# A decoder block in split float32: sums of weights in their quarters' place, four places for split pieces, pairs by sums and plain pairs in turn

## The chip, the core and the metric

The kernel runs on one core of one Trainium2 chip. The core has engines with queues of their own: TensorE (PE in the profile) multiplies matrices, VectorE (DVE), ScalarE (ACT) and GpSimd (POOL) work element by element, and SyncE (SP) starts most of the transfers from HBM. The metric is the device time of one execution in microseconds, and the output must agree with the reference.

## The reference

One layer of a decoder on 256 tokens of 2048 features, all in float32: a feed-forward network (FFN), a mixer of two kinds of attention, and a second FFN, each with a norm ahead and a norm behind it.

```
D_MODEL = 2048
SEQ = 256
D_FF = 5632

def swiglu(x, w_gate, w_up, w_down):
    return (jax.nn.silu(x @ w_gate) * (x @ w_up)) @ w_down

f = swiglu(rmsnorm(x, ffn1_pre_g[l]), ffn1_w_gate[l], ffn1_w_up[l], ffn1_w_down[l])
x = x + FFN_RES_SCALE * rmsnorm(f, ffn1_post_g[l])
h = rmsnorm(x, mix_pre_g[l])
proj = h @ w_in[l]
...
x = x + rmsnorm(o @ w_out[l], mix_post_g[l])
f = swiglu(rmsnorm(x, ffn2_pre_g[l]), ffn2_w_gate[l], ffn2_w_up[l], ffn2_w_down[l])
x = x + FFN_RES_SCALE * rmsnorm(f, ffn2_post_g[l])
```

The change is about the last product of `swiglu`, hidden features (5632) times `w_down`, and about how every weight reaches PE.

## The kernel before, in words

**Split operands.** PE multiplies in a rounded 32-bit format, fp32r. To keep float32 accuracy each operand is split into a high part (the value rounded to fp32r) and a low part (the rest), and three products are added up: high by high, high by low, low by high. The weights are split on the chip. The class `Weights` keeps a list of blocks of 1 MB, each loaded by SP into a ring of three `raw` tiles (`RAW`), and a list of pieces of 1024 columns (in all) per partition. `split_next` makes one piece: ACT copies it to `whi` (line 136), DVE subtracts to `wlo` (line 141). There is a ring of three places for them (`PARTS`), so that piece n can be split only when piece n-3 has been multiplied; `get(i)` asks for splits up to i + 2 and for loads up to two blocks ahead.

**Gate and up.** For each of 22 pairs of feature blocks the weights are PE's stationary operand and the 256 tokens (high and low side by side, 512 columns) its moving one; a piece is 8 matmuls of 512 columns and 8 of 256. Short steps on ACT and DVE, held in a list `todo` and run one entry after each piece (`step`), join the two halves, apply the gate, and split the result for the next product.

**Down.** This product is done in two halves of 11 pairs of feature blocks each, and in each half in two column pairs (2 x 512 of the 2048 output columns). `Down.run` goes through the pairs. A plain pair is two pieces, each of 12 matmuls of 512 columns: 24 for the pair. Four pairs of each half, those in `BY_SUMS`, go by a scheme with seven products in place of eight (a form of Strassen's): the 2 x 2 blocks of hidden features and of weights are added and subtracted, and 21 matmuls do the pair. Their weights come in four pieces, with 6, 3, 6 and 6 matmuls; two of these are sums of the four quarters of a raw block, made on DVE (lines 102, 106, 110) into two tiles of their own, `sum..0` and `sum..1`. `TERMS` says which of the seven sums (of hidden features) meets which quarter and which product bank it goes to. After the last pair by sums, `middle` puts the seven products together on DVE and ACT; after the last pair `finish` adds the plain banks. The second column pair of the second half ends in a tail, in which the last three pairs go one column chunk after the other, so that the norm behind it can begin (`handover`), and the next stage's weights are already split while PE works off held pieces (`take_over`). In these stretches between `ordered()` and `order.close()` the order on the engines is as the program writes it. Elsewhere a scheduler puts each engine's instructions in order by when it believes them to be ready; on the chip each engine then works its queue off strictly in that order.

**Slots.** `slots` is a set of 30 tiles of 4 KB per partition that activations, sums and intermediate results take and give back.

Of the kernel before, what the change touches and what calls it, by code (L numbers as in the profile page):

```python
# [10 lines left out]
F32 = mybir.dt.float32  # L11
# [6 lines left out]
P = 128  # L18
# [8 lines left out]
CH = 512  # L27
# [33 lines left out]
class Weights:  # L61

    RAW, PARTS, WIDTH = 3, 3, 1024

    def __init__(self, nc, pool):
        self.nc, self.pool = nc, pool
        self.blocks, self.raw, self.pieces, self.parts = [], {}, [], {}
        self.loaded = self.split = 0  # L70
        self.sums = None

    def block(self, w, k0, nk, c0, cols, step=None):
        src = w[k0 * P:(k0 + nk) * P, c0:c0 + cols].rearrange("(k p) f -> p k f", p=P)
# [17 lines left out]
    def add_sums(self, w, k0, c0):  # L92


        b = self.block(w, k0, 2, c0, 2 * CH)
        quarters = lambda raw: raw.rearrange("p k (c f) -> p (k c) f", c=2)
        ends = lambda raw: quarters(raw)[:, 0::3]
        eng = self.nc.vector

        def first(raw):  # L100
            t = self.sums[0]
            eng.tensor_sub(t, ends(raw), quarters(raw)[:, 1:2].to_broadcast([P, 2, CH]))

        def second(raw):
            t, u = self.sums
            eng.tensor_add(u[:, 0], quarters(raw)[:, 3], t[:, 0])

        def third(raw):
            u = self.sums[1]
            eng.tensor_sub(u[:, 1], quarters(raw)[:, 2], u[:, 0])  # L110

        return [
            self.piece(b, 2, CH, ends, first),
            self.piece(b, 1, CH, lambda raw: quarters(raw)[:, 2:3], second),
            self.piece(b, 2, CH, lambda raw: self.sums[0], third),
            self.piece(b, 2, CH, lambda raw: self.sums[1], None),
        ]

    def load_to(self, i):
# [54 lines left out]


A11, A12, A22, S1, S3, S2, S4 = range(7)
TERMS = (((0, A11, "1"), (1, S4, "3")), ((0, A12, "2"),), ((0, S1, "5"), (1, S3, "7")), ((0, S2, "6"), (1, A22, "4")))

PLAIN = (("2", "3"), ("4", "X"))

BY_SUMS = (0, 2, 5, 7)
KP = KF // 4


# [1 line left out]
def hybrid_layer(ctx: ExitStack, tc: tile.TileContext, a):  # L186
    nc = tc.nc
    const = ctx.enter_context(tc.tile_pool(name="const", bufs=1))
    slots = Slots(ctx.enter_context(tc.tile_pool(name="slots", bufs=1)), 30)
    wpool = ctx.enter_context(tc.tile_pool(name="wpool", bufs=2))  # L190
    tmp = ctx.enter_context(tc.tile_pool(name="tmp", bufs=2))
    psum = ctx.enter_context(tc.tile_pool(name="psum", bufs=8, space=bass.MemoryType.PSUM))
# [4 lines left out]
    W = Weights(nc, wpool)  # L197
    todo = deque()

    def step():  # L200

        if todo:
            run_all(todo.popleft())
# [34 lines left out]
    def plan_down(n, half, w):  # L238


        for u in range(2):
            end = KP - 3 if (half, u) == (1, 1) else KP
            plan["down", n, half, u] = []
            for p in range(end):
                k, c0 = 2 * (half * KP + p), u * 2 * CH
                plan["down", n, half, u].append((p, W.add_sums(w, k, c0) if p in BY_SUMS else W.add(w, k, 2, c0, 2 * CH)))
        if half == 1:
# [79 lines left out]
    def row_gain(name):  # L327
        g = a[name]
        t = const.tile([P, D], F32, tag="rows", name=f"r_{name}")
        tc.keep_in_program_order(  # L330
            nc.sync.dma_start(t, bass.AP(tensor=g.tensor, offset=g.offset, ap=[[0, P], [1, D]])))
        return t
# [367 lines left out]
    def ffn(n, pre, row_name, end_of):  # L700
# [4 lines left out]
        def put_h(p, f, u, g):  # L705

            if p % KP not in BY_SUMS:
                if f == 0:
# [98 lines left out]
        class Down:  # L807


            def __init__(self, half, u):  # L810
                self.half, self.c = half, (2 * u, 2 * u + 1)
                self.ps, self.done = {}, {}
                self.pairs = plan["down", n, half, u]
                sums = len(BY_SUMS)
                self.n = {x: 3 * sums for x in "1234567"}
# [25 lines left out]
            def run(self):  # L841
                for p, ids in self.pairs:
                    q = self.half * KP + p
                    for m, i in enumerate(ids):
                        part = W.get(i)
                        if p in BY_SUMS:
                            self.sums(*hx[q], part, TERMS[m])
                        else:
                            for t in range(NT):
                                self.plain(hx[q][:, m], part, 0, t)  # L850
                        step()
                    if p == BY_SUMS[-1]:
                        self.middle()
                    if self.c[0]:
                        slots.give(*([f"hi{n}_{q}", f"ho{n}_{q}"] if p in BY_SUMS else [f"h{n}_{q}"]))

# [46 lines left out]

        for half in range(2):
            for fp in range(half * KP, (half + 1) * KP):
                if fp % KP == KP - 1:
                    W.sums = [slots.take([P, 2, CH], F32, f"sum{n}{half}{m}") for m in range(2)]
                gate_up(fp)
            if half == 0:
                post = Post(f"f{n}", row_gain(row_name), half=True)  # L910
            else:
                slots.give(*pre.names)
                more = [slots.take([P, 2, CH], F32, f"more{n}{m}") for m in range(2)]
            for u in range(2):
                d = Down(half, u)
                d.run()
                if (half, u) != (1, 1):
                    for c, t in ((1, 0), (0, 0), (0, 1), (1, 1)):
                        d.finish(c, t)
            slots.give(*(f"sum{n}{half}{m}" for m in range(2)))  # L920
        d.tail(end_of(post))
        slots.give(*(f"more{n}{m}" for m in range(2)), *(f"h{n}_{KF // 2 - 3 + m}" for m in range(3)))
        return post
# [11 lines left out]
    def end_f1(post):  # L935
        return handover(post, next_pre("pre", G[:, G_MIXPRE:G_MIXPRE + KD], "mix", post))

    post1 = ffn(1, pre1, "ffn1_post_g", end_f1)


# [233 lines left out]
    def end_f2(post):  # L1174
# [26 lines left out]
        return end  # L1201

    ffn(2, mix["pre2"], "ffn2_post_g", end_f2)


# [26 lines left out]
```

## Time and profile before

| what | value |
|---|---|
| time, median of 3 runs (lowest, highest) | 1900.07 us (1899.29, 1900.13) |
| the profiled execution: its time, its span | 1898.98 us, 1897.2 us |
| PE busy, matmuls | 1863.5 us (98 %), 9802 |
| DVE busy | 1336.7 us (70 %) |
| ACT busy | 968.6 us (51 %) |
| POOL busy | 105.1 us (6 %) |
| read from HBM | 350 MB, 186 GB/s over the span |
| mean granted clock of PE | 0.995 |

The span runs from the first to the last instruction of the profiled execution; its time is a little longer, and the medians are of other executions. Busy shares are means over the whole span. Matmuls overlap in the record (one of 512 columns is listed with about 0.39 us and starts some 0.23 us after the one before), so lost time on PE is read from starts. In a row of a timeline the bracket at the end gives the idle time of the engine just ahead of the row and what ended it.

### The profile page before, as it was taken

Reading aid. Unit: us, or ns where it says so; the run is one execution under the profiler, and the core shown is the slowest. Engines: PE = TensorE matmul, PEld = TensorE weight load, DVE = VectorE, ACT = ScalarE, POOL = GpSimd, SP = SyncE. Lnnn points to the kernel's source line nnn. Section 1 sums busy time; section 2 is a strip of 40 time slices with the busy share of each in tenths; the row PEclk is TensorE's granted clock in tenths of the full one; section 3 lists DMA queues with packets and bytes.
Section 4 is the critical chain, followed back from the end, with each engine's and each line's share of the span. In section 5 each row is a group of like instructions: output and inputs, shape, how many; then the busy total and the mean of one; then the engine's idle time right before and its main releaser. Section 6 shows DMA issues by size and latency. Waiting matters only on the chain.

```text
span 1897.2 us, 25219 instructions
## 1 busy us (share of the span) xinstructions
PE 1863.5 (98%) x9802; PEld 1590.2 (84%) x9802; DVE 1336.7 (70%) x1966; ACT 968.6 (51%) x1411; POOL 105.1 (6%) x92
## 2 busy tenths in 40 slices
PE   9999999999999998999999998999999999999997
PEld 8888887888888776788888887888887788888875
DVE  6666688766666788656786558766688766666797
ACT  6444455444444555655555446544454544444554
POOL 0000000000000001100353003000000000000001
PEclk9999999999999999999999999999999999999999
DMA  7556565556565554555545555555555655555563
GB/s 252 194 181 196 180 220 196 193 187 195 183 197 181 199 198 145 187 173 168 163 158 171 189 173 177 178 194 185 192 208 188 210 187 191 184 194 185 187 205 112
DMA packets 260120, 353.73 MB, mean 186 GB/s; under 512 B 5856, under 2 KB 219040, under 8 KB 259616
## 3 DMA queue, kind: packets, MB, share of 16 engines
q1 hardware_dynamic: 259552, 351.30, 55.9%
q8 instruction: 77, 1.26, 0.3%
q0 software_dynamic: 272, 0.75, 0.1%
q14 instruction: 43, 0.35, 0.1%
q10 hardware_dynamic: 176, 0.07, 0.0%
HBM read 350.00 MB, written 2.10 MB: 186 GB/s over the span
## 4 chain that ended last, share of the span: by engine, by line
PE 89%; DVE 8%; ACT 2%; issue 1%; POOL 0%; DMA 0%; DVEq 0%; ACTq 0%; POOLq 0%
PE p L496 34%; PE p L505 17%; PE d L825 16%; PE pq L496 5%; PE pw L515 4%; PE pv L515 4%; DVE wlo L141 3%; PE d_X L825 3%; PE pq L505 3%; ACT whi L136 1%; DVE xn L676 1%; DVE fg_f L877 1%; PE po L1026 0%; PE xt_f L459 0%; ACT sqd L368 0%
## 5 line engine op out<-in xcount | busy, mean ns | idle before, releaser
L141 DVE TENSOR_TENSOR wlo<-raw,whi 128x1024 fp32r<-128x1024 f32 (+1 forms) x653 | 784.0, 1205 | 464.5 <-ACT whi L136 452.2
L136 ACT CAST whi<-raw 128x1024 fp32r<-128x1024 f32 (+1 forms) x657 | 674.9, 1028 | 715.1 <-PE p L496 355.6
L496 PE MATMUL p<-xg_f,whi 128*128 128x512 f32 x2784 | 699.1, 392 | 0.0
L496 PEld LDWEIGHTS p<-xg_f,whi 128*128 128x128 f32 x2784 | 500.3, 189 | 89.2
L505 PEld LDWEIGHTS p<-xg_f,wlo 128*128 128x128 f32 x2816 | 384.7, 190 | 27.6
L505 PE MATMUL p<-xg_f,wlo 128*128 128x256 f32 x2816 | 393.8, 282 | 0.0
L825 PE MATMUL d<-whi,h 128*128 128x512 f32 x672 | 211.3, 390 | 0.0
L825 PEld LDWEIGHTS d<-whi,h 128*128 128x128 f32 x672 | 126.1, 188 | 27.0
L496 PE MATMUL pq<-xg_mix,whi 128*128 128x512 f32 x512 | 131.8, 399 | 0.0
L825 PE MATMUL d<-wlo,h 128*128 128x512 f32 x336 | 115.4, 392 | 2.4 <-DVE wlo L141 2.4
L141 DVE TENSOR_TENSOR wlo<-sum,whi 128x1024 fp32r<-128x1024 f32 x64 | 78.3, 1223 | 50.7 <-ACT whi L136 49.8
L496 PEld LDWEIGHTS pq<-xg_mix,whi 128*128 128x128 f32 x512 | 92.2, 189 | 16.9
L136 ACT CAST whi<-sum 128x1024 fp32r<-128x1024 f32 x64 | 67.4, 1052 | 71.7 <-PE d_X L825 46.2
L515 PE MATMUL pv<-whi,xg_mix 128*128 128x512 f32 x256 | 84.3, 400 | 1.7 <-ACT xg_mix L425 1.7
L825 PE MATMUL d_X<-whi,h 128*128 128x512 f32 x224 | 85.6, 389 | 0.0
L655 ACT COPY right<-p 128x256 f32<-128x256 f32 x176 | 60.2, 370 | 43.4 <-DVE u L657 43.4
L825 PE MATMUL d<-wlo,hi 128*128 128x512 f32 x224 | 76.6, 412 | 1.5 <-DVE wlo L141 0.8
L825 PEld LDWEIGHTS d<-wlo,h 128*128 128x128 f32 x336 | 62.0, 188 | 18.9 <-DVE wlo L141 5.1
L515 PE MATMUL pw<-whi,om 128*128 128x512 f32 x256 | 75.1, 391 | 0.0
L505 PEld LDWEIGHTS pq<-xg_mix,wlo 128*128 128x128 f32 x512 | 69.8, 190 | 5.3
L825 PE MATMUL d<-whi,ho 128*128 128x512 f32 x224 | 72.1, 391 | 0.0
L825 PE MATMUL d<-whi,hi 128*128 128x512 f32 x224 | 71.8, 390 | 0.0
(199 smaller groups left out, 1569.9 us busy)
## 6 DMA issues: line engine op xcount, KB each, us to landing
raw<-in_ffn_w_down_dram SPq DMA_DIRECT2D x86, 1024.0 KB, 4.9
raw<-in_ffn_w_gate_dram SPq DMA_DIRECT2D x84, 1024.0 KB, 5.1
raw<-in_ffn_w_up_dram SPq DMA_DIRECT2D x84, 1024.0 KB, 5.1
raw<-in_w_in_dram SPq DMA_DIRECT2D x48, 1024.0 KB, 5.2
raw<-in_w_out_dram SPq DMA_DIRECT2D x16, 1024.0 KB, 5.0
raw<-in_ffn_w_up_dram SPq DMA_DIRECT2D x8, 512.0 KB, 3.8
raw<-in_ffn_w_gate_dram SPq DMA_DIRECT2D x7, 512.0 KB, 3.6
xn<-in_x_dram SPq DMA_DIRECT2D x8, 256.0 KB, 6.1
```

What stands on the lines that cost most here:

```text
L136: self.nc.scalar.copy(hi, raw)
L141: eng.tensor_sub(lo[:, k0:k1], raw[:, k0:k1], hi[:, k0:k1].bitcast(F32))
L496: nc.tensor.matmul(p, wh, x, start=k == 0, stop=False)
L505: nc.tensor.matmul(p[:, :T], lo[:, j, f * P:(f + 1) * P], xs(k)[:, 0, :], start=False, stop=k == KD - 1)
L515: nc.tensor.matmul(ps[c], y, w[:, j, c * CH:(c + 1) * CH], start=first and n == 0, stop=last and n == 2)
L655: nc.scalar.copy(t, ps[:, T:])
L676: nc.vector.scalar_tensor_tensor(x, f, self.z[t], x, op0=ALU.mult, op1=ALU.add)
L825: nc.tensor.matmul(self.ps[x], y, w, start=m == 1, stop=m == self.n[x])
L877: nc.vector.tensor_add(f, self.ps[PLAIN[t][c]], f)
```

## The change

Three things change together. The sums of weights are written into the quarters of the raw block itself (q0 - q1 into q0, q3 - q1 into q1, then q3 + q0 into q3, and q2 - q3 into q2), so the two `sum` tiles and their slots go: 28 slots are left. The operation over two quarters becomes two over one. The third piece now reads quarters 0 and 1, the fourth quarters 2 and 3, which turns round the two terms of the last piece. The space freed is given to a fourth place in the ring of split pieces: piece n waits for piece n-4, and `get` asks for splits up to i + 3. And `BY_SUMS` becomes 0, 2, 4, 6 in place of 0, 2, 5, 7.

```
-    RAW, PARTS, WIDTH = 3, 3, 1024
+    RAW, PARTS, WIDTH = 3, 4, 1024
...
         b = self.block(w, k0, 2, c0, 2 * CH)
         quarters = lambda raw: raw.rearrange("p k (c f) -> p (k c) f", c=2)
-        ends = lambda raw: quarters(raw)[:, 0::3]
         eng = self.nc.vector

         def first(raw):
-            t = self.sums[0]
-            eng.tensor_sub(t, ends(raw), quarters(raw)[:, 1:2].to_broadcast([P, 2, CH]))
+            q = quarters(raw)
+            eng.tensor_sub(q[:, 0], q[:, 0], q[:, 1])
+            eng.tensor_sub(q[:, 1], q[:, 3], q[:, 1])

         def second(raw):
-            t, u = self.sums
-            eng.tensor_add(u[:, 0], quarters(raw)[:, 3], t[:, 0])
-
-        def third(raw):
-            u = self.sums[1]
-            eng.tensor_sub(u[:, 1], quarters(raw)[:, 2], u[:, 0])
+            q = quarters(raw)
+            eng.tensor_add(q[:, 3], q[:, 3], q[:, 0])
+            eng.tensor_sub(q[:, 2], q[:, 2], q[:, 3])

         return [
-            self.piece(b, 2, CH, ends, first),
+            self.piece(b, 2, CH, lambda raw: quarters(raw)[:, 0::3], first),
             self.piece(b, 1, CH, lambda raw: quarters(raw)[:, 2:3], second),
-            self.piece(b, 2, CH, lambda raw: self.sums[0], third),
-            self.piece(b, 2, CH, lambda raw: self.sums[1], None),
+            self.piece(b, 2, CH, lambda raw: quarters(raw)[:, :2], None),
+            self.piece(b, 2, CH, lambda raw: quarters(raw)[:, 2:], None),
         ]
...
-TERMS = (((0, A11, "1"), (1, S4, "3")), ((0, A12, "2"),), ((0, S1, "5"), (1, S3, "7")), ((0, S2, "6"), (1, A22, "4")))
+TERMS = (((0, A11, "1"), (1, S4, "3")), ((0, A12, "2"),), ((0, S1, "5"), (1, S3, "7")), ((0, A22, "4"), (1, S2, "6")))
...
-BY_SUMS = (0, 2, 5, 7)
+BY_SUMS = (0, 2, 4, 6)
...
-    slots = Slots(ctx.enter_context(tc.tile_pool(name="slots", bufs=1)), 30)
+    slots = Slots(ctx.enter_context(tc.tile_pool(name="slots", bufs=1)), 28)
...
-                if fp % KP == KP - 1:
-                    W.sums = [slots.take([P, 2, CH], F32, f"sum{n}{half}{m}") for m in range(2)]
                 gate_up(fp)
...
-            slots.give(*(f"sum{n}{half}{m}" for m in range(2)))
```

What stands in DVE's queue in the first column pair of the first down stretch, before; pieces 99 and 100 are a plain pair, 101 and 102 the next plain pair's, 103 to 106 the third pair by sums:

```order
L141 TENSOR_TENSOR wlo99_2628<-raw51_2575,whi99_2627 128x1024
L141 TENSOR_TENSOR wlo100_2638<-raw51_2575,whi100_2637 128x1024
L141 TENSOR_TENSOR wlo101_2648<-raw52_2612,whi101_2647 128x1024
L102 TENSOR_TENSOR sum100_2282<-raw53_2651 128x1024
L106 TENSOR_TENSOR sum101_2283<-raw53_2651,sum100_2282 128x512
L141 TENSOR_TENSOR wlo102_2666<-raw52_2612,whi102_2665 128x1024
L110 TENSOR_TENSOR sum101_2283<-raw53_2651,sum101_2283 128x512
L141 TENSOR_TENSOR wlo103_2682<-raw53_2651,whi103_2681 128x1024
L141 TENSOR_TENSOR wlo104_2701<-raw53_2651,whi104_2700 128x512
L141 TENSOR_TENSOR wlo105_2718<-sum100_2282,whi105_2717 128x1024
L102 TENSOR_TENSOR sum100_2282<-raw55_2722 128x1024
L141 TENSOR_TENSOR wlo106_2731<-sum101_2283,whi106_2730 128x1024
```

And in the same place in the changed kernel, where pieces 101 to 104 are the third pair by sums and 105 and 106 plain:

```order
L138 TENSOR_TENSOR wlo99_2625<-raw51_2581,whi99_2624 128x1024
L138 TENSOR_TENSOR wlo100_2632<-raw51_2581,whi100_2631 128x1024
L138 TENSOR_TENSOR wlo101_2642<-raw52_2616,whi101_2641 128x1024
L138 TENSOR_TENSOR wlo102_2654<-raw52_2616,whi102_2653 128x512
L101 TENSOR_TENSOR raw52_2616<-raw52_2616 128x512
L102 TENSOR_TENSOR raw52_2616<-raw52_2616 128x512
L106 TENSOR_TENSOR raw52_2616<-raw52_2616 128x512
L107 TENSOR_TENSOR raw52_2616<-raw52_2616 128x512
L138 TENSOR_TENSOR wlo103_2674<-raw52_2616,whi103_2673 128x1024
L138 TENSOR_TENSOR wlo104_2690<-raw52_2616,whi104_2689 128x1024
L138 TENSOR_TENSOR wlo105_2702<-raw53_2659,whi105_2701 128x1024
L138 TENSOR_TENSOR wlo106_2709<-raw53_2659,whi106_2708 128x1024
```

Before, sums stood between low parts, and some ahead of their own pair's first low part; now the four stand in one block, behind the first two low parts of their pair.

DVE's queue in the handover to the mixer before, where `xg_mix` are the mixer's inputs, transposed and split, and `xn` the updated tokens that PE transposes:

```order
L676 SCALAR_TENSOR_TENSOR xn_74<-fg_f12_2503,rs_post_f10_6449,xn_74 128x512
L676 SCALAR_TENSOR_TENSOR xn_74<-fg_f12_2503,rs_post_f11_6482,xn_74 128x512
L141 TENSOR_TENSOR wlo302_6641<-raw139_6522,whi302_6640 128x1024
L426 SCALAR_TENSOR_TENSOR xg_mix4_6464<-xt_mix20_6654,G_97,xg_mix4_6464 128x256 x2
L426 SCALAR_TENSOR_TENSOR xg_mix5_6465<-xt_mix21_6659,G_97,xg_mix5_6465 128x256 x2
L141 TENSOR_TENSOR wlo303_6679<-raw140_6561,whi303_6678 128x1024
```

And in the changed kernel:

```order
L673 SCALAR_TENSOR_TENSOR xn_74<-fg_f12_2507,rs_post_f10_6461,xn_74 128x512
L673 SCALAR_TENSOR_TENSOR xn_74<-fg_f12_2507,rs_post_f11_6494,xn_74 128x512
L138 TENSOR_TENSOR wlo302_6653<-raw139_6534,whi302_6652 128x1024
L138 TENSOR_TENSOR wlo303_6661<-raw140_6573,whi303_6660 128x1024
L423 SCALAR_TENSOR_TENSOR xg_mix4_6476<-xt_mix20_6670,G_97,xg_mix4_6476 128x256 x2
L423 SCALAR_TENSOR_TENSOR xg_mix5_6477<-xt_mix21_6675,G_97,xg_mix5_6477 128x256 x2
```

The low part of piece 303 has moved ahead of the four operations that give the low parts of the mixer's inputs.

## Rows read from the trace of the kernel before

**Rows 1.** The page's first part: busy time, share of the span, instructions.

```profile
PE 1863.5 (98%) x9802; PEld 1590.2 (84%) x9802; DVE 1336.7 (70%) x1966; ACT 968.6 (51%) x1411; POOL 105.1 (6%) x92
```

**Rows 2.** Windows: stretch, length, busy us of PE, PEld, DVE, ACT, POOL; PEclk, DMA, GB/s.

```profile
258.84:376.48 117.64, 117.11 (x506) 93.15 (x505) 94.41 (x102) 60.72 (x66) 0.00 (x0) 1.00 0.57 196
376.48:622.27 245.79, 245.79 (x1410) 216.31 (x1408) 158.92 (x231) 118.42 (x169) 0.00 (x0) 1.00 0.58 189
622.27:741.43 119.16, 117.75 (x506) 93.10 (x504) 103.75 (x126) 64.92 (x80) 1.32 (x2) 1.00 0.56 194
1401.23:1518.97 117.74, 117.26 (x507) 93.21 (x505) 94.38 (x102) 60.72 (x66) 0.00 (x0) 1.00 0.57 196
1764.75:1883.93 119.18, 117.76 (x506) 93.12 (x504) 103.69 (x127) 62.91 (x78) 1.29 (x1) 1.00 0.49 167
```

**Rows 3.** Timeline of PE: first matmul of five plain pieces, and of what follows.

```profile
304.14 0.61 PE L825 MATMUL d<-whi,h 128*128 128x512 f32 x2
...
317.74 0.62 PE L825 MATMUL d<-whi,hi 128*128 128x512 f32 x2
```

**Rows 4.** Timeline of PE: where it waits in down stretches, and a sums pair's start.

```profile
258.84 0.63 PE L825 MATMUL d<-whi,hi 128*128 128x512 f32 x2
...
265.06 0.73 PE L825 MATMUL d<-wlo,h 128*128 128x512 f32 x2 [0.37 <-DVE wlo L141]
...
269.73 0.62 PE L825 MATMUL d<-whi,hi 128*128 128x512 f32 x2
...
271.77 0.61 PE L825 MATMUL d<-whi,hi 128*128 128x512 f32 x2
272.34 0.73 PE L825 MATMUL d<-wlo,hi 128*128 128x512 f32 x2
...
684.23 0.74 PE L825 MATMUL d<-wlo,hi 128*128 128x512 f32 x2 [0.40 <-DVE wlo L141]
...
736.08 0.50 PE L825 MATMUL d<-wlo,h 128*128 128x512 f32 x1 [0.49 <-DVE wlo L141]
```

**Rows 5.** Timelines of ACT and DVE: the split behind the wait at 272.34.

```profile
269.97 1.05 ACT L136 CAST whi<-sum 128x1024 fp32r<-128x1024 f32 x1 [2.10 <-DVE sum L106]
...
271.06 2.59 DVE L141 TENSOR_TENSOR wlo<-sum,whi 128x1024 fp32r<-128x1024 f32 x2 [0.38 <-ACT whi L136]
```

**Rows 6.** Groups by form (busy, mean ns), and two low parts in a row.

```profile
L141 DVE TENSOR_TENSOR wlo<-raw,whi 128x1024 fp32r<-128x1024 f32 x26 | 31.2, 1221 | 2.9 <-ACT whi L136 2.1
L102 DVE TENSOR_TENSOR sum<-raw 128x1024 f32<-128x1024 f32 x6 | 7.3, 1221 | 0.1
L141 DVE TENSOR_TENSOR wlo<-raw,whi 128x512 fp32r<-128x512 f32 x7 | 4.8, 690 | 3.2 <-ACT whi L136 3.2
L106 DVE TENSOR_TENSOR sum<-raw,sum 128x512 f32<-128x512 f32 x7 | 4.8, 688 | 0.1
...
L711 DVE TENSOR_TENSOR u<-u,g 128x256 f32<-128x256 f32 x56 | 23.6, 422 | 0.8
...
265.25 2.36 DVE L141 TENSOR_TENSOR wlo<-raw,whi 128x1024 fp32r<-128x1024 f32 x2
```

**Rows 7.** The page's DMA issues: count, size, median us to landing.

```profile
raw<-in_ffn_w_down_dram SPq DMA_DIRECT2D x86, 1024.0 KB, 4.9
```

**Rows 8.** Timelines of POOL, DVE, ACT and PE in the handover to the mixer.

```profile
740.08 3.65 POOL L141 TENSOR_TENSOR wlo<-raw,whi 128x512 fp32r<-128x512 f32 x2 [736.62 <-DVE rs_post_f L352]
...
741.61 2.67 DVE L141 TENSOR_TENSOR wlo<-raw,whi 128x512 fp32r<-128x512 f32 x1
...
756.73 1.05 ACT L136 CAST whi<-raw 128x1024 fp32r<-128x1024 f32 x1 [1.06 <-PE pv L515]
...
759.46 3.53 DVE L676 SCALAR_TENSOR_TENSOR xn<-fg_f,rs_post_f,xn 128x512 f32<-128x512 f32 x2
...
763.04 0.98 PE L459 MATMUL xt_mix<-ident,xn 128*128 128x128 f32 x7 [1.72 <-DVE xn L676]
```

## What was predicted, and how it was worked out

> **What bounds the kernel now.** First the page's busy line: TensorE (PE) is busy 1863.5 of 1897.2 us [rows 1]. As its matmuls overlap in the record, that share does not say how much time is lost, so I read stretches second. In the gate/up stretch between two down stretches PE is busy 245.79 of 245.79 us: nothing to win there [rows 2]. The four down stretches (the two halves of each FFN's down projection) last 117.64, 119.16, 117.74 and 119.18 us, 473.72 us together [rows 2]. Each holds 504 matmuls of 512 columns: two column pairs of 4 x 21 + 7 x 24. (The windows count two or three more, from neighbours that overlap the edge.) Five pieces of a plain run without a wait, 60 matmuls, go from 304.14 to 317.74 us, 0.2267 us each [rows 3]. 4 x 504 x 0.2267 = 457.0 us, so the four stretches lose 16.8 us to something other than matmuls: 3.4, 4.9, 3.5 and 4.9 us. That is the most that any edit to the supply of split pieces can give back here.
>
> Third, the timeline of PE, to see where it is lost. PE stops in front of a matmul that reads wlo: 0.37 us at 265.06 (0.53 us over its pitch, with the restart), 0.12 us at 272.34 (0.57 us after the pair at 271.77, where two matmuls take 0.45), 0.40 us at 684.23, 0.49 us at 736.08 [rows 4]. So each loss is a low part (VectorE, DVE) that comes late. Why late: at 269.97 ScalarE (ACT) starts the high part of a sums piece after 2.10 us without work, and DVE's two low parts follow at 271.06, in 2.59 us [rows 5]. PE wanted the first of them 2.04 + 0.45 us after the pair's start at 269.73, at 272.2; it got it at 272.3. DVE is not out of time (94.41 of 117.64 us in that stretch, [rows 2]): the piece may only be split when its place in the ring is free, two pieces ahead.
>
> **The change, part by part.**
>
> *Matmuls.* The same 9802, the same shapes; only which pair comes when, and the fourth piece takes its two quarters the other way round. 0 us.
>
> *Sums in place.* Per pair by sums, one 1024-element subtraction (1.22 us) and two of 512 (0.69 us each) become four of 512: 4 x 0.688 = 2.75 us against 2.60 [rows 6]. 32 such pairs: 5 us more DVE work in the whole kernel, on an engine with 94 of 118 us taken. Hidden by PE's matmuls as long as DVE keeps its lead; with that cover gone it costs 5 us. The Trainium skill ("VectorE: DVE Perf Modes", Rules for kernel authors) speaks against this part: it asks to minimise the number of DVE operations, since each pays a fixed cost. The rows above agree on the price (two halves 0.16 us over one whole); by the rule alone the sum would be 12.2 - 4.8 = 7.4 us and 1892.7, by the rows it is 1887.9, since DVE is last only in places.
>
> The raw block of such a pair is now held until its fourth piece is split (before: until the third sum). Loads of it take 4.9 us [rows 7].
>
> *Four places.* Piece n is split when n-4 has been multiplied, not n-3. Take the alternation from the start of a sums pair at 0: pieces of 6, 3, 6, 6 matmuls start at 0, 1.36, 2.04, 3.40; the plain pair's two at 4.76 and 7.48; the next sums pair at 10.2. Places for the next sums pair come free at 3.4, 4.8, 7.5 and 10.2. ACT needs 1.05 us for a high part [rows 5], DVE 1.22 for a low part [rows 6]. The plain pieces' low parts are done near 3.7 and 4.9, the first sums piece's at 6.1, the second's at 6.8, the four sums at 9.6, the third's low part at 10.8, where PE wants it at 10.2 + 2.04 + 0.45 = 12.7; the fourth's at 12.5, wanted at 14.1. Before, the third's place came free at 10.2, and its low part was due at 12.5 at best. So the steady waits at third and fourth pieces go. DVE's work per such double pair is 3 x 1.22 + 0.69 + 2.75 + 2 x 1.22 = 9.5 of 10.2 us: enough, with little to catch up with.
>
> *The order of pairs.* 0, 2, 4, 6 instead of 0, 2, 5, 7: four double pairs in a row at 9.5 of 10.2 us, then four plain pairs at 2.4 of 5.4. What is late when such a run begins stays late for long. Two places: (a) the first column pair of a half begins while DVE still closes the last gate/up. On the clock of [rows 4], with the pair's start at 258.84: the fourth sums piece's low part ends at 258.84 + 1.05 + 1.22 = 261.1. Behind it in DVE's queue stand eight gate/up operations (0.42 us), three low parts of 1.22, one of 0.69, four sums (0.69), and then the second sums pair's third low part [rows 6]. End to end that is 10.5 us, and the low part ends at 272.8; but two low parts in a row take 2.36, not 2.44 us [rows 6], and 16 such overlaps of 0.08 make it 271.5. PE wants it at 269.1 + 2.04 + 0.45 = 271.6. Between none and 1.2 us late I take 0.35, plus 0.1 for the restart. Four times, 1.8 us, in place of the 0.53 + 0.11 us at 265.06, where the plain piece's low part now comes at 264.0 to 264.4 for 264.1. (b) In the second halves the second column pair begins with eight 0.69 us operations (adds, then gains). Counted in the same way, with 0 at its start, the fourth piece's low part comes at 3.8 for 3.9, the plain piece's at 5.5 for 5.2, and after four sums the next third piece's at 13.5 for 12.7 + 0.3: 0.3 + 0.1 and 0.6 + 0.1 us with restarts, with a little for what drags behind 1.4, twice: 2.8 us. (In the first halves only the four adds stand there, 2.75 us, and the same count leaves over 1 us of lead.) The end of the second halves gains: the sums' results are put together one pair earlier, and the fourth place lets the last piece be split before the column's adds; the 0.49 us at 736.08 goes, and its like in the other FFN.
>
> *Gate/up and the mixer.* Here the order of ACT and DVE is that of before with every split one piece later in number, so each stands where it stood in PE's time; the streams wait nowhere in [rows 2]. 0 us, and bounds of -0.3 and +0.3 for the two places where a row broadcast moves by a few matmuls.
>
> *The handovers.* In the one to the mixer the fourth place frees the split that waited 1.06 us for PE at 756.73; behind it stand the two xn updates at 759.46 and PE's transposes at 763.04, 1.72 us idle [rows 8]. That comes up to 1 us earlier. But the order now puts one more whole low part (wlo303, 1.22 us) ahead of the mixer's x columns on DVE, and PE has about 1 us in hand there. -0.9 + 1.0: I count 0, bounds -1 and +2 (below).
>
> **Sum.** 16.8 - 1.8 - 2.8 = 12.2 us gained. Of the profiled execution (span 1897.2, its own time 1898.98): 1886.8. The median is 1900.07, 1.09 above it: **1887.9 us**.
>
> **Rivals.**
>
> 1. *The waits come back in DVE's queue.* The four sums now stand in one block ahead of a low part, and 9.5 of 10.2 us is near the edge; 7 % more per operation and every sums pair is late again. For it: the list above with margins of 0.1 to 0.3 us. Against: the margins grow after the second pair, and plain pairs give 3 us each. Then only what is not steady goes: 0.64 at four starts, 1.0 at two second column pairs (684.23 and what follows), 0.76 at two tails: 6.1 us, 1894.
>
> 2. *VectorE and GpSimd in the handover.* While POOL works at 740.08 (3.65 us), DVE's 512-element low part at 741.61 takes 2.67 us, alone 0.69; the two updates at 759.46 take 3.53 [rows 8]. Mechanism: the added low part meets POOL's updates of xn, takes 2.0 us more than alone, and PE waits for the x columns behind it: 12.2 - 2 = 10.2 us gained, 1889.9. The Trainium skill ("SBUF — State Buffer", Who interferes with whom) says that the port pair of the two is an exclusive lock, so that the later one blocks fully; the 2.67 us agree.
>
> 3. *Slower: the ring of raw blocks.* It still has three places, and a sums block is held some 7 us longer (until its last split; the splits themselves come 2.7 us earlier). In the alternation a sums block is free at 2.3 and a plain one at 4.8 of each 10.2 us; the loads land by 7.2 and 9.7 and are wanted at 11.6 and 13.6: 4 us in hand with 4.9 us per load. Only if two that overlap took over 9 us each would PE wait: to come out slower it has to lose 12.2 + 3.8 = 16 us, 0.5 us at each of 32 sums pairs, 1904 or more. Against: DMA engines at 0.57 of their time in these stretches [rows 2].
>
> 4. *It does not help.* The late part is late for another reason (the sums themselves, at 269.97 ACT's wait ended on a sum): two waits for one, within 3.8 us, 1897 to 1900. Against: the sums are now made from 6.8 to 9.6, ahead of the place.
>
> **Numbers.** Forecast 0.66 (own range 1883.3, nothing left of the 16.8, to 1891), rival 1 0.13, rival 2 0.12, rival 3 0.04, rival 4 0.05. A measurement of this kernel tells about 0.2 %, 3.8 us. Faster: forecast, rivals 1 and 2, 0.91, less a little for a rival 1 with more behind it: 0.90; same 0.06; slower 0.04. The range leaves out 3, 4 and the outer half of 1: 1884 to 1893.5.
>
> **What would show it.** The four down stretches 114.3 us plus 0.5 (first halves) and 1.9 (second); PE's waits for wlo at third pieces of the second sums pair and after the second column pair of second halves, none elsewhere; no DMA among the releasers of ACT; the gate/up stretch at 245.8 us as before; PE's wait near 763 shorter and perhaps a new one for the x columns behind it. Wrong it is if the down stretches still lose over 2 us each in first halves (rival 1), if ACT's splits wait for DMA (rival 3), or if the time goes outside the down stretches.

## The result, and the profile after

The changed kernel takes **1886.34 us** (median of 4 runs, 1886.25 to 1886.46) against 1899.68 (1898.63 to 1900.13) for the kernel before, measured with it: ratio 0.9931, 95% interval 0.9913 to 0.9948. Predicted were 1887.9, within 1884 to 1893.5. The profiled execution took 1886.46 us, its span is 1884.4 (before: 1898.98 and 1897.2). One execution of e10 below took 2627.99 us, at a mean granted clock of 0.653, and is left out of its figures.

First the page's busy line of the kernel after, the counterpart of [rows 1].

```profile
PE 1853.7 (98%) x9802; PEld 1595.8 (85%) x9802; DVE 1342.1 (71%) x1998; ACT 965.5 (51%) x1411; POOL 103.0 (5%) x92
```

PE has the same 9802 instructions, DVE 32 more and 5.4 us more work, and the kernel is still 13 us shorter. The windows over the same five stretches as in [rows 2] show where:

```profile
258.97:373.24 114.27, 114.27 (x506) 94.61 (x505) 95.46 (x109) 60.26 (x66) 0.00 (x0) 1.00 0.58 208
373.24:619.02 245.78, 245.78 (x1409) 216.31 (x1408) 159.16 (x232) 118.53 (x169) 0.00 (x0) 1.00 0.56 186
619.02:734.49 115.47, 114.83 (x506) 94.17 (x504) 103.78 (x132) 63.01 (x79) 1.35 (x2) 1.00 0.56 201
1395.61:1509.88 114.27, 114.27 (x507) 94.60 (x505) 95.47 (x109) 60.28 (x66) 0.00 (x0) 1.00 0.58 207
1755.66:1871.16 115.50, 114.86 (x506) 94.17 (x504) 103.75 (x133) 61.13 (x77) 1.29 (x1) 1.00 0.48 173
```

In the first halves PE is busy from end to end: 114.27 us, against 504 x 0.2267 = 114.25 that the matmuls alone take. The second halves still lose 1.2 us each. The four together went from 473.72 to 459.51, so 14.2 us were gained; the gate/up stretch is what it was. The span fell by 12.7 only. From the first xt_mix transpose to the first pr_mix matmul (the mixer's handover and its first projection) PE takes 42.27 us where it took 40.15: 2.1 given back. The way into FFN 2 gave 0.7, the rest about nothing.

What the second halves still lose stands in PE's timeline of the kernel after, at the second column pair:

```profile
688.64 0.64 PE L822 MATMUL d<-whi,hi 128*128 128x512 f32 x2
689.92 0.50 PE L822 MATMUL d<-whi,hi 128*128 128x512 f32 x1 [0.64 <-ACT whi L133]
```

After the third piece's first two matmuls, which take 0.45, PE stands 0.81 us longer. It waits for the high part of the fourth piece: in this column pair the scheduler has put the first matmul of the fourth piece ahead of the third's low part. ACT's rows, with the third piece's split and then the fourth's, and DVE's rows in front of them:

```profile
687.37 1.05 ACT L133 CAST whi<-raw 128x1024 fp32r<-128x1024 f32 x1 [4.07 <-DVE raw L102]
688.82 3.90 ACT L133 CAST whi<-raw 128x1024 fp32r<-128x1024 f32 x4 [0.40 <-PE d L822]
```

```profile
675.92 1.88 DVE L874 TENSOR_TENSOR fg_f<-d,fg_f 128x512 f32<-128x512 f32 x3
677.72 0.68 DVE L874 TENSOR_TENSOR fg_f<-d_X,fg_f 128x512 f32<-128x512 f32 x1
678.32 0.69 DVE L684 TENSOR_TENSOR fg_f<-fg_f,r_ffn_post_g 128x512 f32<-128x512 f32 x1
678.92 1.22 DVE L138 TENSOR_TENSOR wlo<-raw,whi 128x1024 fp32r<-128x1024 f32 x1
680.05 0.68 DVE L684 TENSOR_TENSOR fg_f<-fg_f,r_ffn_post_g 128x512 f32<-128x512 f32 x1
...
685.87 0.68 DVE L101 TENSOR_TENSOR raw<-raw 128x512 f32<-128x512 f32 x1
686.59 0.69 DVE L102 TENSOR_TENSOR raw<-raw 128x512 f32<-128x512 f32 x1
687.31 0.69 DVE L106 TENSOR_TENSOR raw<-raw 128x512 f32<-128x512 f32 x1
688.04 0.69 DVE L107 TENSOR_TENSOR raw<-raw 128x512 f32<-128x512 f32 x1
688.65 3.61 DVE L138 TENSOR_TENSOR wlo<-raw,whi 128x1024 fp32r<-128x1024 f32 x3
```

ACT is idle for 4.07 us and waits for the sum of L102, then again until the sum of L107 ends at 688.73; its split ends at 689.87, where PE goes on. (The last row names PE as the releaser, whose last matmul before it ended at about the same time; in the first column pairs the same row names DVE's L107.) The third piece's low part, the first of the three at 688.65, takes 1.22 us and ends at 689.87 too, so in the usual order PE would have waited as long, for that one. The sums come so late because DVE had four adds and four gains (L684) to do first. No place of the ring decides here.

The handover, counterpart of [rows 8], in the rows of POOL, DVE, ACT and PE of the kernel after, and its windows at the end:

```profile
749.49 1.28 POOL L138 TENSOR_TENSOR wlo<-raw,whi 128x512 fp32r<-128x512 f32 x1 [0.19 <-ACT whi L133]
751.88 2.40 POOL L138 TENSOR_TENSOR wlo<-raw,whi 128x1024 fp32r<-128x1024 f32 x1 [1.12 <-ACT whi L133]
754.24 3.39 POOL L676 TENSOR_TENSOR xn<-xn,fg_f 128x512 f32<-128x512 f32 x2
...
749.87 1.45 DVE L138 TENSOR_TENSOR wlo<-raw,whi 128x512 fp32r<-128x512 f32 x1
...
752.28 4.23 DVE L673 SCALAR_TENSOR_TENSOR xn<-fg_f,rs_post_f,xn 128x512 f32<-128x512 f32 x2
756.42 3.43 DVE L138 TENSOR_TENSOR wlo<-raw,whi 128x1024 fp32r<-128x1024 f32 x2
759.77 1.65 DVE L423 SCALAR_TENSOR_TENSOR xg_mix<-xt_mix,G,xg_mix 128x256 fp32r<-128x256 f32 x4
...
748.33 1.06 ACT L133 CAST whi<-raw 128x1024 fp32r<-128x1024 f32 x1
...
754.89 0.33 PE L456 MATMUL xt_mix<-ident,xn 128*128 128x128 f32 x1 [0.85 <-DVE xn L673]
756.56 0.98 PE L456 MATMUL xt_mix<-ident,xn 128*128 128x128 f32 x7 [1.34 <-DVE xn L673]
...
755.00:757.50 2.50, 1.16 (x9) 0.97 (x10) 2.50 (x2) 0.36 (x1) 2.50 (x2) 1.00 0.28 109
757.50:761.00 3.50, 3.50 (x10) 2.71 (x9) 3.50 (x6) 2.32 (x6) 0.13 (x1) 0.51 0.29 64
```

The same two steps in POOL's and DVE's timelines of the kernel before:

```profile
757.87 1.79 POOL L141 TENSOR_TENSOR wlo<-raw,whi 128x512 fp32r<-128x512 f32 x1 [1.52 <-ACT whi L136]
759.84 2.60 POOL L141 TENSOR_TENSOR wlo<-raw,whi 128x1024 fp32r<-128x1024 f32 x1 [0.18 <-ACT whi L136]
...
757.81 0.69 DVE L141 TENSOR_TENSOR wlo<-raw,whi 128x512 fp32r<-128x512 f32 x1 [0.81 <-ACT whi L136]
```

The split at 748.33 no longer waits; before, it waited 1.06 us. The low part of its piece is made in two halves, one on POOL and one on DVE. Measured from the four transposes ahead of it (at 756.48 before, 749.31 now), DVE's half starts 0.56 us behind them instead of 1.33. But the updates of xn (752.28) did not come earlier by the same measure (2.97 for 2.98), though DVE has no idle time between. Before, DVE's half began 0.06 us ahead of POOL's and took 0.69; now POOL's half is 0.38 ahead, and DVE's takes 1.45. That took back what the earlier split had gained. The next step repeats it: before, POOL's second low part began at 759.84, 0.38 us after DVE's first update (759.46, [rows 8]); now it begins 0.40 us ahead of it. The first update waits behind it, the second behind POOL's own add at 754.24: 4.23 us for two instead of 3.53, and PE waits 0.85 + 1.34 instead of 1.72. Then both low parts of L138 (3.43 us) stand in front of the x columns. PE would want these about 3 us after the transposes, but the granted clock is 0.51 (the lower of the two levels, 1.2 GHz) from 757.5 to 761, so that wait does not show here: nine matmuls each take 0.20 us more.

### The profile page after: what moved, and what is told of

Its sections match the earlier page's. It is cut to its first block, busy times and chain, and to the rows that moved or that the text cites. A ratio compares the mean times of both kernels' runs of the same rounds, so it can differ in the third digit from the quotient of the medians.

```text
span 1884.4 us, 25317 instructions
## 1 busy us (share of the span) xinstructions
PE 1853.7 (98%) x9802; PEld 1595.8 (85%) x9802; DVE 1342.1 (71%) x1998; ACT 965.5 (51%) x1411; POOL 103.0 (5%) x92
## 4 chain that ended last, share of the span: by engine, by line
PE 94%; DVE 4%; ACT 1%; issue 1%; POOL 0%; DMA 0%; DVEq 0%; ACTq 0%; POOLq 0%
PE p L493 34%; PE d L822 20%; PE p L502 18%; PE pq L493 5%; PE pw L512 4%; PE pv L512 4%; PE d_X L822 4%; PE pq L502 3%; DVE wlo L138 1%; DVE xn L673 1%; PE po L1020 0%; PE xt_f L456 0%; ACT sqd L365 0%; PE p L497 0%; ACT whi L133 0%
## 5 line engine op out<-in xcount | busy, mean ns | idle before, releaser
L138 DVE TENSOR_TENSOR wlo<-raw,whi 128x1024 fp32r<-128x1024 f32 (+1 forms) x717 | 859.3, 1209 | 487.5 <-ACT whi L133 482.3
L133 ACT CAST whi<-raw 128x1024 fp32r<-128x1024 f32 (+1 forms) x721 | 736.9, 1030 | 768.5 <-PE p L493 374.7
L822 PE MATMUL d<-whi,h 128*128 128x512 f32 x672 | 207.5, 389 | 0.0
L822 PE MATMUL d<-wlo,hi 128*128 128x512 f32 x224 | 71.8, 390 | 0.0
L502 PE MATMUL pq<-xg_mix,wlo 128*128 128x256 f32 x512 | 71.3, 282 | 0.0
L138 POOL TENSOR_TENSOR wlo<-raw,whi 128x512 fp32r<-128x512 f32 (+1 forms) x10 | 17.8, 1786 | 824.2 <-DVE rs_post_f L349 729.7
```

The source lines that it names most:

```text
L133: self.nc.scalar.copy(hi, raw)
L138: eng.tensor_sub(lo[:, k0:k1], raw[:, k0:k1], hi[:, k0:k1].bitcast(F32))
L502: nc.tensor.matmul(p[:, :T], lo[:, j, f * P:(f + 1) * P], xs(k)[:, 0, :], start=False, stop=k == KD - 1)
L822: nc.tensor.matmul(self.ps[x], y, w, start=m == 1, stop=m == self.n[x])
```

## The experiments

Eleven kernels ran, in three series whose runs of the kernel before had medians of 1899.11 (e1 to e4), 1898.92 (e5 to e8) and 1898.99 us. The table has the medians, the ratio to the kernel before with its interval, and stretches of each profiled execution, by the starts of PE's matmuls: A the first half of FFN 1; B the second half of FFN 1 up to the first xt_mix (some 3.7 us longer than the window above); C from there to pr_mix; C2 the part of C behind its fourth group of transposes (from 749.66 us in the kernel after); D the second half of FFN 2.

| kernel | us | ratio (95%) | A | B | C | C2 | D |
|---|---|---|---|---|---|---|---|
| before | 1899.68 | | 117.64 | 122.93 | 40.15 | 28.52 | 119.18 |
| after | 1886.34 | 0.9931 (0.9913-0.9948) | 114.27 | 119.16 | 42.27 | 30.79 | 115.50 |
| e1 three places | 1901.63 | 1.0012 (1.0002-1.0021) | 117.67 | 123.75 | 41.44 | 28.81 | 119.95 |
| e2 old order | 1886.57 | 0.9935 (0.992-0.9949) | 114.27 | 119.43 | 42.49 | 30.16 | 115.45 |
| e3 in place alone | 1903.99 | 1.0025 (1.0014-1.0036) | 117.67 | 125.15 | 41.61 | 28.84 | 121.17 |
| e4 four raw blocks | 1901.85 | 1.0012 (1.0003-1.0022) | 117.70 | 123.72 | 41.59 | 28.80 | 120.01 |
| e5 handover | 1884.01 | 0.9921 (0.9907-0.9934) | 114.27 | 119.17 | 41.38 | 28.71 | 115.49 |
| e6 gains later | 1885.93 | 0.9930 (0.9917-0.9942) | 114.27 | 119.02 | 42.79 | 30.20 | 115.36 |
| e7 one operation | 1885.58 | 0.9931 (0.9917-0.9944) | 114.27 | 118.97 | 42.88 | 30.12 | 115.27 |
| e8 all | 1881.59 | 0.9908 (0.9895-0.9922) | 114.27 | 119.02 | 39.95 | 27.57 | 115.31 |
| e9 no gains | 1882.77 | 0.9915 (0.9902-0.9929) | 114.27 | 117.97 | 41.98 | 30.12 | 114.27 |
| e10 x first | 1885.57 | 0.9929 (0.9916-0.9943) | 114.27 | 119.18 | 42.26 | 30.79 | 115.47 |
| e11 best | 1881.78 | 0.9908 (0.9893-0.9923) | 114.27 | 118.96 | 39.25 | 27.57 | 115.26 |

Totals carry noise that no edit touches: the first down starts between 257.94 and 259.19 us in these profiles, with the code in front of it the same. C is disturbed too: its first 40 matmuls, ahead of C2, take 11.47 to 12.79 us, by how long the granted clock stays low there (0.98 from 743.69 to 749.66 us in the kernel after, 0.80 from 743.13 to 750.30 in e5, the same 31 matmuls). So I read stretches first, and C2 ahead of C.

### Which of the three parts does it: e1, e2, e3

e1 is the changed kernel with three places.

```diff
-    RAW, PARTS, WIDTH = 3, 4, 1024
+    RAW, PARTS, WIDTH = 3, 3, 1024
```

> The changed kernel with three places for split pieces again (sums in place and strict turns kept). Theory A, the fourth place makes the gain: the third piece of each pair by sums is split only when PE begins the pair, its low part comes about 0.1 us late with 0.1 us of restart, and the waits at the starts of column pairs return: down stretches near 117.5 and 119 us, time 1897 to 1902 us. Rival B, the even turns of pairs make the gain (VectorE is loaded evenly): down stretches near 114.5 and 116 us, 1886 to 1890 us.

e2 keeps four places and takes the pairs in the order of before.

```diff
-BY_SUMS = (0, 2, 4, 6)
+BY_SUMS = (0, 2, 5, 7)
```

> The changed kernel with the pairs by sums at 0, 2, 5, 7 again (four places and sums in place kept). Theory A: the down stretches keep nearly all of their gain (114.3 in first halves, 115.5 to 116.5 in second ones, where the assembly of the seven products falls next to the tail again), time 1886 to 1889 us. Rival B, the even turns: about half of the gain goes, 1892 us or more.

e3 has both of these edits: of the change only the sums in place are left.

> Only the sums in place (three places, pairs by sums at 0, 2, 5, 7): one 512-element operation more per pair by sums on VectorE, and the sums can only be made after the first low part of their block. Theory A: 1898 to 1903 us, nothing gained. Rival C, the place of the sums (no separate tiles to wait for) makes the gain: below 1893 us.

With three places A is 117.67 us, as before the change, in both orders; with four it is 114.27 in both. So the fourth place is the whole gain: 15.3 us from e1 to the kernel after. The sums in place alone cost 4.9 us (e3 against its own runs of before; 1 us above the range expected), mostly in B and D (C2 grows by 0.3 only); the new order gives 2.4 of that back, but with four places it is worth nothing (e2). Four places beside separate tiles for the sums were not run, so that the sums in place do no more than make the room is not shown. How three places lose is seen in PE's, ACT's and DVE's timelines of e1, at the second sums pair of A:

```profile
271.82 0.61 PE L822 MATMUL d<-whi,hi 128*128 128x512 f32 x2
272.64 0.50 PE L822 MATMUL d<-whi,hi 128*128 128x512 f32 x1 [0.21 <-ACT whi L133]
...
271.54 2.00 ACT L133 CAST whi<-raw 128x1024 fp32r<-128x1024 f32 x2 [0.40 <-DVE raw L107]
...
267.95 0.69 DVE L138 TENSOR_TENSOR wlo<-raw,whi 128x512 fp32r<-128x512 f32 x1 [0.28 <-ACT whi L133]
268.56 0.69 DVE L101 TENSOR_TENSOR raw<-raw 128x512 f32<-128x512 f32 x1
```

DVE waits for the second piece's split, which waits for its place; the four sums start at 268.56, and the fourth piece's split at 271.54 ends at 272.59, where PE goes on. The pair's first matmul stands at 269.78, so the sums start 1.2 us ahead of it. In the kernel after they start at 267.17 for a pair at 269.20, 2.0 us ahead, and nothing waits.

### Is it the raw blocks: e4

```diff
-    RAW, PARTS, WIDTH = 3, 4, 1024
+    RAW, PARTS, WIDTH = 4, 3, 1024
```

> The space of the fourth place given to a fourth raw block instead (three places for split pieces, four raw blocks, sums in place, strict turns). Theory A: as with three places and three raw blocks, 1897 to 1902 us, since no split waits for a load. Rival D, the loads of raw blocks set when splits begin: 1888 us or less.

The same memory given to a fourth raw block buys nothing: every stretch is within 0.2 us of e1 in the table. Loads do not set the splits; the depth that counts is that of the split pieces.

### The handover: e5, e10

e5 takes GpSimd's second low part and its two adds out of this step; its half of the low part before them stays.

```diff
-        W.split_next()[0](nc.gpsimd)
+        low = W.split_next()[0]
         pre.update(2, 0)
         pre.update(2, 1)
+        low(nc.vector)
         mm(2, parts[2], 1)
+        pre.update(3, 0)
+        pre.update(3, 1)
         W.split_to(ids[0] + 5)
-        pre.update(3, 0, nc.gpsimd)
-        pre.update(3, 1, nc.gpsimd)
```

> Where two VectorE updates of xn ran beside a low part and two adds of GpSimd in both handovers after an FFN, GpSimd now has nothing: the low part stands on VectorE behind the two updates, and the two later updates of xn are VectorE's too. Theory A (contention of VectorE and GpSimd is what the mixer's handover lost): the two updates take 1.4 us in place of 4.23, PE does not wait for xn, and the stretch from the first xt_mix to pr_mix goes from 42.27 to 40.0 to 41.0 us; in all 1.0 to 2.5 us less than the changed kernel, 1884.0 to 1885.4. Rival B (the one more low part ahead of the x columns is what it lost): PE's wait for xn goes, but the same time comes back as a wait for xg_mix a few us later, stretch 41.8 to 42.5, total within 0.5 us of 1886.3. The down stretches as in the changed kernel (114.3 and 115.5 to 119.2 us).

DVE's and PE's timelines of e5:

```profile
752.99 1.40 DVE L674 SCALAR_TENSOR_TENSOR xn<-fg_f,rs_post_f,xn 128x512 f32<-128x512 f32 x2
...
756.77 2.35 DVE L138 TENSOR_TENSOR wlo<-raw,whi 128x1024 fp32r<-128x1024 f32 x2
759.04 1.65 DVE L423 SCALAR_TENSOR_TENSOR xg_mix<-xt_mix,G,xg_mix 128x256 fp32r<-128x256 f32 x4
...
754.52 1.03 PE L456 MATMUL xt_mix<-ident,xn 128*128 128x128 f32 x8
...
759.57 1.12 PE L512 MATMUL pv<-whi,xg_mix 128*128 128x512 f32 x3 [1.70 <-DVE xg_mix L423]
```

Without GpSimd the two updates take 1.40 us, as expected, and PE's waits for xn are gone. But 1.70 us come back a little later as a wait for the x columns, behind the two low parts. So theory A was right on the cause and rival B on what comes next. C fell by 0.9 us, between the two, but its first 40 matmuls took 1.2 us longer than in the kernel after, at a lower clock; C2 fell by 2.1, and by 1.4 against e7, which has the handover of the kernel after but not the lower clock in its C2. The step that e5 edits stands in the handover to FFN 2 as well: from pr_mix to FFN 2's first down e5 takes 614.43 us, the kernel after 615.16. DVE's half beside POOL's still takes 1.78 us; no kernel without that was run.

e10 moves only the second of these low parts behind the x columns.

```diff
-            part = W.get(ids[m][1])
+            part = W.get(ids[m][1], 2 if rest and m == 3 else W.PARTS - 1)
```

> Only the second low part in front of the mixer's x columns moves behind them; GpSimd keeps its part. Theory A (contention delays the xn updates, and the low part is a second, separate loss that shows only once the first is gone): PE still waits 0.8 and 1.3 us for xn, the stretch from the first xt_mix to pr_mix is 41.5 to 42.8 us, total 1885.3 to 1886.5. Rival B (the low part is what the handover lost): the stretch falls to 40.2 to 41.2 us, total 1884.3 to 1885.3, without touching GpSimd.

PE still waits for xn (1.04 and 1.56 us over its pitch), the granted clock falls behind it as in the kernel after, and C is 42.26: alone this edit gives nothing in the profile, as theory A had it. The four runs took 1884.85, 1885.00, 1886.13 and 1886.65 us, so part of them gained; the profile is of the slowest, and what differs in the others stays open.

### The adds and gains: e6, e9, e7

e6 puts the four gains of the second halves' first column pair off to later steps.

```diff
+                later((4, 10, 16, 25)[n], lambda: nc.vector.tensor_mul(self.fg[c][:, t], src, self.row(c)))
```

> The four multiplications by the row gain, which stand on VectorE at the start of the second column pair of a second half, are spread one by one over later plain pairs. Theory: their block (with the adds 5.5 us of VectorE's time) is what keeps the 1.1 us in each second half; the waits at that place go, the stretch from the second down of FFN 1 to the first xt_mix falls from 119.16 to 118.1 us, that of FFN 2 (to the end) likewise, total 1884.0 to 1884.6. Rival (the four dependent sums in a row are what is late, whatever stands before them): the 0.81 us stay, total within 0.4 us of 1886.3. Third case: a gain pushed into a later double pair makes a wait there, no gain in all.

The edit did not do what it says: the scheduler put the gains only 3 to 5 us later, two of them among the sums and one right behind the last, as DVE's timeline of e6 shows for the two:

```profile
683.39 0.68 DVE L101 TENSOR_TENSOR raw<-raw 128x512 f32<-128x512 f32 x1
683.99 0.68 DVE L689 TENSOR_TENSOR fg_f<-fg_f,r_ffn_post_g 128x512 f32<-128x512 f32 x1
684.59 0.68 DVE L102 TENSOR_TENSOR raw<-raw 128x512 f32<-128x512 f32 x1
685.20 0.68 DVE L689 TENSOR_TENSOR fg_f<-fg_f,r_ffn_post_g 128x512 f32<-128x512 f32 x1
```

The wait of 0.81 us became two, 0.42 and 0.38 over the pitch. That neither supports nor refutes the theory, so e9 leaves these multiplications out.

```diff
-                if self.half:
+                if self.half and self.c[0] == 0:
+                    post.sq.add(t, self.c[c], f)
+                elif self.half:
                     post.take(t, self.c[c], f)
```

> This one leaves out the multiplication of columns 0 to 1023 of both FFNs' outputs by the row gain (eight VectorE operations of 512 elements in all), since the kernel with the gains put off showed that they were only shifted to among the sums. Theory: with the gains the adds are too much for VectorE's lead at the second column pair of second halves; without them no wait is left there, as in the first halves, where only the adds stand: 119.16 to 118.0 to 118.2 us and 115.50 to 114.3 to 114.5 us, total 1884.0 to 1884.4. Rival (the chain of dependent sums is late by itself): the 0.6 to 0.8 us stay and the total is 1885.6 to 1886.4.

The windows of both second halves of e9:

```profile
618.00:732.27 114.27, 114.27 (x506) 94.44 (x504) 101.60 (x128) 63.31 (x79) 1.36 (x2) 1.00 0.57 203
...
1753.34:1867.60 114.26, 114.26 (x506) 94.41 (x504) 101.48 (x129) 61.44 (x77) 1.29 (x1) 1.00 0.48 175
```

Nothing is lost in any down stretch any more: the gains, on top of the adds, are what was left, 1.2 us twice. (The total fell by more, 3.6 us, of which 1.0 lies ahead of the first down.)

e7 makes one operation of the first two sums again, in place.

```diff
-            eng.tensor_sub(q[:, 0], q[:, 0], q[:, 1])
-            eng.tensor_sub(q[:, 1], q[:, 3], q[:, 1])
+            eng.tensor_sub(q[:, :2], q[:, 0::3], q[:, 1:2].to_broadcast([P, 2, CH]))
```

> The first two sums of a pair are one VectorE operation of 1024 elements, in place, as before the change (1.22 us for 2 x 0.69): one operation fewer in each of 32 pairs, about 5 us of VectorE's time less in all. Theory (VectorE is last only in the second column pair of second halves): 0.1 to 0.3 us there, twice, nothing elsewhere; total 1885.7 to 1886.4. By the rule that each operation's fixed cost is paid in full: about 4.8 us less, 1881.5.

B and D fall by 0.19 and 0.23 us, A does not move: an operation more per pair costs only where DVE is last. The total is 0.76 us lower, within what the front of the program varies by.

### Together: e8, e11

e8 is e5, e6 and e10 together; e11 is e5, e7 and e10.

> The handover without GpSimd's part, the gains spread, and the second of the two low parts in front of the mixer's x columns moved behind them. If the theories on both places hold, the parts add: 1.0 to 2.5 us of the handover, about 2 us of the gains, and up to 1.2 us of the x columns: 1881.3 to 1883.3. If the handover's loss only moves about: 1884.3.

> The handover without GpSimd's part and with the x columns first, and the first two sums as one operation; the gains where the change has them. If the parts are separate: handover 40.0 us, second halves 118.97 and 115.27 us, total 1881.2 to 1881.9, as the kernel with all (1881.59) or a little under it.

DVE's and PE's timelines of e11 in the handover, and its window:

```profile
752.23 1.40 DVE L673 SCALAR_TENSOR_TENSOR xn<-fg_f,rs_post_f,xn 128x512 f32<-128x512 f32 x2
...
757.15 1.65 DVE L422 SCALAR_TENSOR_TENSOR xg_mix<-xt_mix,G,xg_mix 128x256 fp32r<-128x256 f32 x4
...
753.77 1.03 PE L455 MATMUL xt_mix<-ident,xn 128*128 128x128 f32 x8
...
757.68 1.12 PE L511 MATMUL pv<-whi,xg_mix 128*128 128x512 f32 x3 [0.56 <-DVE xg_mix L422]
...
757.50:761.00 3.50, 3.32 (x14) 2.60 (x15) 3.50 (x6) 1.36 (x2) 0.00 (x0) 1.00 0.73 230
```

The x columns begin at 757.15 instead of 759.04 (e5), 0.56 us of the wait is left, the clock stays at 1.00, and C is 39.25 us: 3.0 less than in the kernel after and 0.9 less than before. C2 is 27.57 in e8 and in e11 alike; the 0.7 us between their C are the lower clock at its start. Both versions beat both kernels: 1881.59 and 1881.78 us, 4.8 and 4.6 below the changed kernel by the medians (0.7 to 0.8 of it is what the kernel before differs by between the series). Their intervals of the ratio to the kernel before, up to 0.9922 and 0.9923, just overlap that of the changed kernel, from 0.9913. Which of the two is faster can't be told. Both lie in their ranges, e8 by another way than expected: the gains put off brought 0.1 to 0.2 us in each second half, where about 2 in all were counted, and the handovers more (2.3 us in C, 0.5 on the way to FFN 2).

## Why the prediction was right, and where it was off

**The bound and the ceiling.** Right. The four down stretches lost 16.8 us to late pieces; 14.2 came back, where the sum had 12.2. That the total is nearer than its terms is luck: the 2.0 us more and the 0.7 on the way into FFN 2, which was counted as 0 with bounds of 0.3, stand against 2.1 lost in the handover. The 0.7 come with the fourth place (615.07 to 615.34 us from pr_mix to FFN 2's first down in the kernel after, e2, e6, e7, e9 and e10, with three places 615.66 to 615.88); where, is not followed here.

**Four places.** Right, and it is the only part that gains: without it (e1) the kernel is slower than before, with it the old order does as well (e2). The prediction also took the order to matter and charged it; with four places it costs and gives nothing. (Behind the four double pairs stand three plain pairs, not four; no term of the sum rests on that count.)

**(a), first column pairs, 1.8 us: did not occur.** The step that failed is "with the pair's start at 258.84: the fourth sums piece's low part ends at 258.84 + 1.05 + 1.22 = 261.1". It let the fourth piece's split begin with the pair. ACT's and DVE's timelines of the kernel after:

```profile
258.26 1.05 ACT L133 CAST whi<-raw 128x1024 fp32r<-128x1024 f32 x1 [1.75 <-PE p L493]
...
259.34 1.23 DVE L138 TENSOR_TENSOR wlo<-raw,whi 128x1024 fp32r<-128x1024 f32 x1 [1.57 <-ACT whi L133]
...
269.95 4.77 DVE L138 TENSOR_TENSOR wlo<-raw,whi 128x1024 fp32r<-128x1024 f32 x4
```

The pair starts at 258.97. The last gate/up piece is read high part first; when its matmuls with the low part begin, at 258.02, the place of its high part is free, and the split runs 0.71 us ahead of the pair. So the fourth piece's low part ends at 260.57, 1.6 us behind the pair's start and not 2.3, and the third piece's low part, the first of the row at 269.95, is there by about 271.2; PE takes it at 271.69. It was counted for 271.5 at best.

**(b), second halves, 2 x 1.4 us.** The size was right (1.2 each), the cause too (e9: adds and gains), the link in part. It is one wait, not two: at the plain piece PE loses 0.1 us, where 0.4 was counted. And PE stops for the high part of a fourth piece, which ACT splits right behind the sum of L107, and not for wlo; but the third piece's low part, for which it was to wait, ends at the same 689.87.

**DVE's added work at nothing.** Right to 0.4 us in all (e7). The rule that the Trainium skill states in "VectorE: DVE Perf Modes", Rules for kernel authors, would have made it 4.8: the rule holds for the engine's own time, and here PE hides it.

**The handover counted as -0.9 + 1.0.** This term was mis-sized: C grew by 2.1 us, just past its bound of +2. The -0.9 came out as nothing: DVE's half of the freed piece did start earlier, but now behind POOL's half and not ahead of it, and took 1.45 us for 0.69; and POOL's next low part started ahead of the updates of xn. Rival 2 had the mechanism, in another place: not the added low part met POOL's work, the half piece and the updates did. 1.40 us without POOL (e5) against 4.23 beside it. The Trainium skill ("SBUF — State Buffer", Who interferes with whom) calls this an exclusive lock, and the rows agree: DVE's half ends 0.55 us after POOL's half (751.32 after 750.77), and the two updates end as much after POOL's low part and after its first add. Of the 2.1 us 0.7 are PE's longer waits for xn, and 1.6 the matmuls behind them at the lower clock, less 0.2 at the start of C. Where the clock stays up behind these waits (e2), the added low part shows instead: PE waits 0.48 for the x columns and loses 0.9 in all in that place.

**What would show it.** First halves 114.27 for 114.8, second 115.5 for 116.2, gate/up 245.78 for 245.8. One thing forecast was not so: DMA is among the releasers of ACT, as the waits of ACT from 619 to 734 us show:

```profile
ACT whi L133 <- DMA raw<-in_ffn_w_down_dram: 1.8, 1, 1.8
```

One split waits 1.8 us for its load, and 4.6 in two in e2, without a wait of PE behind it. The loads themselves take 5.0 us at the median, against 4.9 in [rows 7]. Rival 3 named a resource that is near, but did not decide.

## What to carry to other kernels

When a consumer stops for the output of an engine that is idle a third of the time, ask what that engine is waiting for, and find which of several rings sets it: one more split piece gave 15 us, the same memory as one more load block gave nothing. A deeper ring also starts other work earlier, so list what each freed instruction now runs beside: of the 2 us given back in the handover, 0.7 came with two GpSimd operations that had begun 0.06 and 0.38 us behind VectorE's and now began 0.38 and 0.40 us ahead of them. And look at the timeline of an edit that "puts work off" before judging by its time: the scheduler may have put it somewhere else.

## What the runs showed of the hardware

- The four sums of a pair on VectorE, which work in place on one block and use one another's quarters, start 0.72 to 0.73 us apart (685.87, 686.59, 687.31, 688.04 above), independent operations of the same size 0.60 (three in 1.88 us at 675.92). The forecast had 0.69 for both.
- In the handover an operation of VectorE (512 elements) that started while GpSimd was at work ended 0.55 us behind GpSimd's; one that started first was not held up. Of one piece's two halves VectorE's took 0.69 us and GpSimd's 1.79 that way (757.81 and 757.87 above), and 1.45 and 1.28 with GpSimd 0.38 us ahead (749.87 and 749.49).
- The granted clock in the handover is not a function of the last wait alone. In the kernel after, PE is busy for 1.16 of 2.5 us and then has 0.51 for 3.5 us; in e9 it is busy for 1.11 of 2.5 us at the same place and the clock stays at 1.00. In e1, with the same waits as before the change (1.98 and 1.88 us over the pitch), five more matmuls fell into the lower clock after the long wait at the start of C, and C is 1.3 us longer, 1.0 of it ahead of C2. So about a microsecond of a handover's length can be clock that no edit made, and a difference there is safer read from the waits.
